# Token-major query/key products with transposes, later S4/S3 sums and spread row scalings in a two-layer hybrid encoder

## The chip, the cores and the metric

The kernel runs on one core of a Trainium2 chip. The metric is the time of one execution on the device in microseconds (us). A profiled execution gives the trace; its time is told beside its span, which goes from the first to the last instruction.

## What is computed

Two layers of a hybrid encoder work on 512 tokens of 2048 features. In each layer the RMS-normalised tokens go through one input projection. Its columns feed a gated linear attention (GLA, 4 heads, with a low-rank forget gate) and a chunked softmax attention (8 heads). Both results are normalised per head, gated, put side by side and multiplied by one output matrix; that product is normalised and added to the tokens. Cut to what matters:

```python
def hybrid_layer(x, ...):
    z = rmsnorm(x, g_pre) @ w_in
    gq, gk, gv, gg, ga, aq, ak, av, ag = split_columns(z)
    o_gla = rmsnorm(gla_chunk_causal(gq, gk, gv, log_a), g_gla) * silu(gg)
    o_att = rmsnorm(chunk_band_attention(aq, ak, av, rel_bias), g_att) * silu(ag)
    y = concatenate([o_gla, o_att]) @ w_out
    return x + rmsnorm(y, g_post)
```

Everything is float32.

## The kernel before, in words

**Numbers.** Each float32 operand is split into a rounded high part and the rest (`split`, L105/L106; with a scale L109/L110: ACT makes the high part, DVE the rest), and a product is the sum of three matmuls: high x high, high x rest, rest x high.

**Products.** The input projection is cut into blocks of 512 columns. Most go in pairs through `fast_gemm` (L316), which forms four block products from seven (P1 to P7, as Strassen does), each over four chunks of 512 rows: 28 jobs a pair. `PAIRS` (L125) gives the order of pairs: two value blocks of attention (AV), two pairs of query/key blocks (QK01/QK23 and QK45/QK67), GK/GQ, GV and GG of the GLA. Then come the output blocks: W01, the first output pair, in both layers, and W23, as a pair in the last layer (L1352) and as plain blocks in the first. The tables L131 to L133 set the order of a pair's jobs; "52" in them is P5 on chunk 2. P1's, P5's and P6's PSUM results are copied by ACT into `ev` tiles (L333), later products are combined with these by DVE (L338).

**A job.** SP issues the loads of weights (L149, `raw` and `H`) and, where needed, of operand sums (L175, `sa`). DVE adds or subtracts weight halves (L185, L187), ACT casts the high part (`wh`, L191), DVE makes the rest (`wl`, L199). Then PE runs its matmuls: 12 of 512 columns token-major (L381), with tokens as the rows of the result, or 24 of 256 columns feature-major (L371), with features as the rows. Only the two query/key pairs are feature-major, since attention wants features there; `qk_consume` splits their results at once, from `ev` or PSUM.

**Order of work.** Besides the products there are tasks, written as Python generators: attention (`attend`, whose steps L929 lists: scores L853 to L855, softmax on DVE L858, transposes L874, mix L891, gate L916), the forget gate, the GLA, the sums for the output pair, the end of the tokens. After each job `pump` (L249) lets the first task take its next steps, as many as the pair's rate says; `until` (L264) pumps until a condition holds. New tasks go to the end of the list, or to its front. From the program so written a scheduler fixes the order on each engine; `tc.issue_after` keeps an instruction behind another.

**Around the output pairs.** `output_sums` makes the operand sums S1, S2, then S4 and S3 of four chunks each (DVE L1136 or L1153, then a split with L105/L106), and in the last layer writes them to DRAM by POOL's DMA for W23. The wait at L1149 sets when an S4 or S3 may be made. W01's results are scaled by the gain (L1281) and their squares summed on ACT (L1280).

**The end of the last layer.** `finish_token` takes the root (DVE L1296, POOL L421), scales the rows of a token block `t` and adds the old tokens `x_mid`. For `t` = 0 and 1 and the first half of `t` = 2 this is ACT (L1305), an accumulating DMA from POOL's queue (L1306) and an output DMA on SP's queue (L1307). The other pieces are one DVE operation (L1311) and an output DMA on SP's or ACT's queue (L1313).

PSUM holds four tiles for products (`mm`) and four for the rest (`ax`).

Of the kernel before, what the change touches and what calls it, by code (L numbers as in the profile page):

```python
# [15 lines left out]
P = 128  # L16
# [10 lines left out]
QS = 128 ** -0.5  # L27
# [6 lines left out]
def hybrid_trunk(  # L34
# [52 lines left out]
    def aux():  # L87
        return ps_ax.tile([P, 512], F32, tag="ax", name=nm("ax"))
# [224 lines left out]
    A = {}  # L313
    roles = ["XY", "YX"]

    def fast_gemm(l, pair, consume, rate=0.0, skip=0, feature_major=False, after=None, end=False, lag=0, ops=A):  # L316
        b0 = pair[0]
        acc = {n: [ps_mm.tile([P, W], F32, tag="mm", name=nm("mm")) for _ in range(2)] for n in roles[0]}
        roles.reverse()
        target = {"P1": "X", "P5": "Y", "P6": "X", "P3": "Y", "P7": "X", "P2": "Y", "P4": "X"}  # L320
        starts = ["P1", "P5", "P2"]
        if end:
            target.update(P2="Z", P4="Y")
            starts.append("P4")
        prod = (PROD_OUT if b0 == NB_IN else PROD_END) if end else PROD
        pace = Pace(rate, skip)
        keep = {}

        def copies(name, src):
            keep[name] = []  # L330
            for t in range(2):
                e = ev()
                nc.scalar.copy(e, src[t])  # L333
                keep[name].append(e)

        def combine(a, b, op, home):
            def f(dst=home):
                nc.vector.tensor_tensor(out=dst, in0=a, in1=b, op=op)  # L338
                return dst
            return f  # L340

        def finished(k, t):
            x_, y_ = acc["X"][t], acc["Y"][t]
            if k == "P3":
                consume(1, 0, t, None, combine(y_, keep["x"][t], ALU.subtract, keep["x"][t]))
            elif k == "P7":
                consume(1, 1, t, None, combine(keep["p5"][t], x_, ALU.subtract, keep["p5"][t]))
            elif k == "P2":
                consume(0, 0, t, None, combine(acc[target[k]][t], keep["p1"][t], ALU.add, keep["p1"][t]))
            elif k == "P4" and end:  # L350
                consume(0, 1, t, None, combine(y_, keep["x"][t], ALU.add, keep["x"][t]))
            elif k == "P4":
                consume(0, 1, t, x_, None)

        def matmuls(job, k, c, ts):
            a = job.a
            if a is None:
                key = {"P1": (0, 0, c), "P2": (1, 0, c), "P4": (1, 1, c)}.get(k) or (LEFT[k], c)
                until(lambda: key in ops)
                a = ops[key]  # L360
            out_ps = acc[target[k]]
            fresh = k in starts and c == 0
            for kk in range(2):
                if feature_major:
                    for ft in range(4):
                        f = slice(ft * P, (ft + 1) * P)
                        tok = slice(kk * 256, (kk + 1) * 256)
                        dst = out_ps[ft // 2][:, (ft % 2) * 256 : (ft % 2 + 1) * 256]
                        terms = ((job.wh, 0), (job.wh, 1), (job.wl, 0))
                        for m, (lhs, part) in enumerate(terms):  # L370
                            nc.tensor.matmul(  # L371
                                dst, lhs[:, kk, f], a[:, part, tok],
                                start=(fresh and kk == 0 and m == 0 and ft % 2 == 0),
                                stop=(c == 3 and kk == 1 and m == 2), skip_group_check=True,
                            )
                else:
                    for t in ts:
                        tok = slice(kk * 256 + t * P, kk * 256 + (t + 1) * P)
                        terms = ((0, job.wh), (0, job.wl), (1, job.wh))
                        for m, (part, rhs) in enumerate(terms):  # L380
                            nc.tensor.matmul(  # L381
                                out_ps[t], a[:, part, tok], rhs[:, kk, :],
                                start=(fresh and kk == 0 and m == 0),
                                stop=(c == 3 and kk == 1 and m == 2), skip_group_check=True,
                            )
# [302 lines left out]
    def layer(l):  # L688
# [272 lines left out]
               (1, 1): ("g12", "g13", "g14", "g15"), (1, 0): ("g4", "g5", "g6", "g7")}  # L961

        def qk_consume(p):
            sets = {}

            def f(j, h, b, src, comb):
# [5 lines left out]
                hs = slice(h * 256, (h + 1) * 256)  # L972
                hi, lo = sets[j][2 * b][:, :, hs], sets[j][2 * b + 1][:, :, hs]
                if b == 0:
                    split_scaled(hi, lo, z, -QS)
# [8 lines left out]
        fast_gemm(l, PAIRS[1], qk_consume(0), rate=2.1, feature_major=True)  # L984
        fast_gemm(l, PAIRS[2], qk_consume(1), rate=2.1, feature_major=True)

        until(lambda: 0 in heads_done)
        tasks.insert(0, forget_gate_decay())
# [137 lines left out]
        def output_sums():  # L1126
# [19 lines left out]
                        yield  # L1146
            for name in ("S4", "S3"):
                for i in range(4):
                    while (("P5", "P6")[i // 2], i % 2 + 2 * (name == "S3")) not in used or (0, OC[i]) not in og:  # L1149
                        yield  # L1150
                    a11, a12, a21, a22 = parts[OC[i]]
                    if name == "S4":
                        nc.vector.tensor_tensor(out=a12, in0=a12, in1=a22, op=ALU.add)  # L1153
                        put(name, i, a12, f"g{i}")
                    else:
                        sub(a11, a11, a21)
                        put(name, i, a11)
                    yield
# [135 lines left out]
        def finish_token(t, xs):  # L1294
# [5 lines left out]
            for i in range(D // step):  # L1300
                h, o = i * step // 1024, i * step % 1024
                yt = ys[t, h][:, o : o + step]
                rows = slice(t * P, (t + 1) * P), slice(i * step, (i + 1) * step)
                if last and (t < 2 or (t == 2 and i == 0)):
                    nc.scalar.activation(yt, yt, AF.Copy, scale=r)  # L1305
                    nc.gpsimd.dma_start(yt, x_mid[rows], accum_op=ALU.add)  # L1306
                    nc.sync.dma_start(out[rows], yt)  # L1307
                else:
                    xt = piece(xs, i * step, step)
                    with tc.issue_after(reduced[3]) if last and t == 2 else nullcontext():  # L1310
                        nc.vector.scalar_tensor_tensor(out=xt, in0=yt, scalar=r, in1=xt, op0=ALU.mult, op1=ALU.add)  # L1311
# [109 lines left out]
```

## Time and profile before

| what | value |
|---|---|
| median of 3 runs | 1646.22 us (1645.83 to 1648.16) |
| the profiled execution | 1642.34 us |
| its span | 1640.5 us |
| granted TensorE clock, mean | 0.995 |
| PE, DVE, ACT busy | 99%, 76%, 55% |

PE is TensorE, DVE VectorE, ACT ScalarE, POOL GpSimd, SP the engine that issues most DMAs; a "q" behind a name means its queue. A row of the timeline gives start, duration, engine, line, operation, written tile <- read tiles and the count; in brackets stands the idle time of that engine ahead of it and what ended it. A row of groups gives busy time and mean duration in ns. A row of the chain in order of time gives start, length and what the chain ran through. Matmuls are pipelined, so the distance between starts, not the duration of one, is its price.

### The profile page before, as it was taken

To read this page: it belongs to the slowest core of one execution; us is meant where nothing else is said; L and a number is where in the kernel's file an instruction comes from. 1 tells how busy PE (TensorE), PEld (TensorE's weight loads), DVE (VectorE), ACT (ScalarE), POOL (GpSimd) and SP (SyncE) were. 2 spreads that over 40 slices of the span, in tenths; PEclk is the share of its full clock that TensorE was granted. 3 is DMA by queue.
4 is the path that set the end of the run, shared out by engine and by line. 5 is a ranking of instruction groups with operands and counts; after the bars stand their busy time and mean duration, and the time that the engine had idled before them with its cause. 6 is when DMAs were issued, how large, how long until landed. Compare 5 with 4: busy or idle time off the path is not lost.

```text
span 1640.5 us, 24563 instructions
## 1 busy us (share of the span) xinstructions
PE 1617.2 (99%) x8986; PEld 1383.7 (84%) x8986; DVE 1253.5 (76%) x1635; ACT 909.7 (55%) x1498; POOL 134.2 (8%) x196
## 2 busy tenths in 40 slices
PE   9999999999999999999999999999999999999996
PEld 7888999998888778788888889999988877787885
DVE  5977677687787869985786576776777878699876
ACT  7554445566555456654784444455665545476554
POOL 0120000110100110000132000000000001101002
PEclk9999999999999999999999999999999999999998
DMA  9898685885859667486789486858758596786968
GB/s 345 270 357 293 221 302 199 266 298 173 307 192 339 225 220 267 145 296 214 240 282 394 172 311 218 298 189 273 269 183 291 184 327 235 241 282 246 345 224 269
DMA packets 130760, 426.70 MB, mean 260 GB/s; under 512 B 14084, under 2 KB 26756, under 8 KB 130640
## 3 DMA queue, kind: packets, MB, share of 16 engines
q1 hardware_dynamic: 113760, 366.09, 64.9%
q0 software_dynamic: 16304, 57.96, 9.7%
q8 instruction: 71, 1.16, 0.3%
q10 hardware_dynamic: 576, 1.08, 0.2%
q14 instruction: 49, 0.40, 0.1%
HBM read 371.84 MB, written 53.23 MB: 259 GB/s over the span
## 4 chain that ended last, share of the span: by engine, by line
PE 94%; DMA 2%; DVE 2%; issue 1%; ACT 0%; SPq 0%; DVEq 0%; POOL 0%; ACTq 0%
PE mm L381 47%; PE mm L371 19%; PE mm L302 16%; PE ax L891 2%; PE ax L381 2%; DMA raw<-in_w_dram 1%; PE ax L1072 1%; PE ax L874 1%; PE ax L711 1%; PE ax L1044 1%; DVE wl L199 1%; PE ax L855 1%; PE ax L854 1%; PE ax L853 1%; PE ax L1164 0%
## 5 line engine op out<-in xcount | busy, mean ns | idle before, releaser
L381 PE MATMUL mm<-wh,sa 128*128 128x512 f32 x1472 | 479.2, 396 | 1.2 <-ACT wh L191 1.0
L191 ACT CAST wh<-raw 128x1024 fp32r<-128x1024 f32 (+1 forms) x253 | 265.1, 1052 | 242.6 <-PE mm L381 65.2
L199 DVE TENSOR_TENSOR wl<-raw,wh 128x1024 fp32r<-128x1024 f32 (+1 forms) x253 | 306.5, 1216 | 92.7 <-PE mm L381 38.3
L191 ACT CAST wh<-H 128x1024 fp32r<-128x1024 f32 x240 | 251.4, 1050 | 214.8 <-PE mm L381 90.2
L199 DVE TENSOR_TENSOR wl<-H,wh 128x1024 fp32r<-128x1024 f32 x240 | 292.5, 1221 | 88.1 <-PE mm L381 35.8
L381 PEld LDWEIGHTS mm<-wh,sa 128*128 128x128 f32 x1472 | 277.5, 189 | 68.9 <-issue 7.9
L381 PE MATMUL mm<-wl,sa 128*128 128x512 f32 x736 | 289.6, 394 | 4.7 <-DVE wl L199 4.7
L371 PE MATMUL mm<-sa,wh 128*128 128x256 f32 x1280 | 236.7, 285 | 0.0
L381 PE MATMUL mm<-wh,a 128*128 128x512 f32 x608 | 200.5, 394 | 0.0
L371 PEld LDWEIGHTS mm<-sa,wh 128*128 128x128 f32 x1280 | 199.7, 191 | 0.1
L371 PE MATMUL mm<-sa,wl 128*128 128x256 f32 x640 | 181.2, 283 | 0.0
L381 PEld LDWEIGHTS mm<-wl,sa 128*128 128x128 f32 x736 | 139.1, 189 | 33.7 <-DVE wl L199 6.7
L185 DVE TENSOR_TENSOR H<-H,raw 128x1024 f32<-128x1024 f32 x132 | 160.2, 1219 | 8.1 <-DMA raw<-in_w_dram 7.0
L381 PEld LDWEIGHTS mm<-wh,a 128*128 128x128 f32 x608 | 113.2, 188 | 23.3
L187 DVE TENSOR_TENSOR raw<-H,raw 128x1024 f32<-128x1024 f32 x60 | 73.5, 1224 | 68.8 <-DMA raw<-in_w_dram 68.7
L371 PEld LDWEIGHTS mm<-sa,wl 128*128 128x128 f32 x640 | 122.5, 191 | 0.2
L421 POOL TENSOR_TENSOR sm<-sm,mhalf 128x2 f32<-128x2 f32 (+2 forms) x42 | 57.1, 1360 | 791.8 <-DVE sm L901 453.3
L381 PE MATMUL mm<-wl,a 128*128 128x512 f32 x304 | 119.8, 394 | 0.0
L371 PE MATMUL mm<-a,wh 128*128 128x256 f32 x512 | 95.2, 285 | 0.0
L302 PE MATMUL mm<-wh,a 128*128 128x512 f32 x288 | 91.7, 390 | 0.0
L381 PE MATMUL mm<-wh,g 128*128 128x512 f32 x288 | 90.8, 389 | 0.0
L333 ACT COPY ev<-mm 128x512 f32<-128x512 f32 x96 | 56.0, 583 | 56.3 <-PE mm L381 39.5
(237 smaller groups left out, 2428.5 us busy)
## 6 DMA issues: line engine op xcount, KB each, us to landing
raw<-in_w_dram SPq DMA_DIRECT2D x323, 512.0 KB, 4.8
sa<-S SPq DMA_DIRECT2D x184, 512.0 KB, 4.4
H<-in_w_dram SPq DMA_DIRECT2D x60, 512.0 KB, 4.6
sa<-A SPq DMA_DIRECT2D x48, 512.0 KB, 5.9
S<-g POOLq DMA_DIRECT2D x32, 512.0 KB, 9.0
sa<-oS SPq DMA_DIRECT2D x16, 512.0 KB, 4.5
oa<-g POOLq DMA_DIRECT2D x12, 512.0 KB, 6.6
bias<-in_rel_dram SPq DMA_DIRECT2D x16, 256.0 KB, 4.2
```

The costliest lines, as they stand in the source:

```text
L185: nc.vector.tensor_tensor(out=h, in0=h, in1=r, op=ALU.add)
L187: nc.vector.tensor_tensor(out=r, in0=h, in1=r, op=ALU.subtract)
L191: last_cast[0] = nc.scalar.copy(self.wh[:, z, :], src[:, z, :]).ins
L199: nc.vector.tensor_tensor(out=self.wl[:, z, :], in0=self.src[:, z, :], in1=self.wh[:, z, :].bitcast(F32), op=ALU.subtract)
L302: nc.tensor.matmul(pss[o], a(part, kk, o) if callable(a) else a[:, part, t], rhs[:, kk, :], start=(i == 0 and kk == 0 and m == 0), stop=(i ...
L333: nc.scalar.copy(e, src[t])
L371: nc.tensor.matmul(dst, lhs[:, kk, f], a[:, part, tok], start=(fresh and kk == 0 and m == 0 and ft % 2 == 0), stop=(c == 3 and kk == 1 and ...
L381: nc.tensor.matmul(out_ps[t], a[:, part, tok], rhs[:, kk, :], start=(fresh and kk == 0 and m == 0), stop=(c == 3 and kk == 1 and m == 2), ...
L421: nc.gpsimd.tensor_tensor(out=out_r, in0=v, in1=mhalf[:, : v.shape[-1]], op=ALU.pow)
L711: nc.tensor.matmul(ps[0:96, half * 256 : (half + 1) * 256], wga[kt // 10][:, kt % 10, :], op[:, i, (kt % 2) * 256 : (kt % 2 + 1) * 256], s ...
L853: nc.tensor.matmul(ps[:, :n], self.qh[:, t], self.kh[:, :n], start=True, stop=False)
L891: nc.tensor.matmul(o, self.pt[i][:, j * P : (j + 1) * P], av[hd // 4, j // 2][:, j % 2, (hd % 4) * P : (hd % 4 + 1) * P], start=(j == 0), ...
```

## The change

It has three parts.

1. The feature-major form is gone. The query/key pairs are computed token-major, like the rest (L368 of the changed kernel). When both token tiles of a block half are there, a new task `turn_qk`, put at the front of the list, waits one step, transposes them with 8 PE transposes into two `ax` tiles, and splits from these. A P4 result, which has no combine, is first copied by ACT into an `ev` tile, 8 copies in all. Attention's task is appended by `turn_qk`, so it starts later.
2. In `output_sums` the wait of S4 and S3 names other jobs: S4 of chunk i waits for P2 on chunk 2 and 3 and P5 on chunk 2 and 3 in turn, S3 besides for P3 on its chunk.
3. In `finish_token` of the last layer the pieces of `t` = 0 and 1 wait three steps each and their ACT scaling stands behind the latest weight cast; the first half of `t` = 2 goes the way of DVE.

```diff
-    def fast_gemm(l, pair, consume, rate=0.0, skip=0, feature_major=False, after=None, end=False, lag=0, ops=A):
+    def fast_gemm(l, pair, consume, rate=0.0, skip=0, after=None, end=False, lag=0, ops=A):
...
-                if feature_major:
-                    for ft in range(4):
-                        f = slice(ft * P, (ft + 1) * P)
-                        tok = slice(kk * 256, (kk + 1) * 256)
-                        dst = out_ps[ft // 2][:, (ft % 2) * 256 : (ft % 2 + 1) * 256]
-                        terms = ((job.wh, 0), (job.wh, 1), (job.wl, 0))
...
+            def turn_qk(j, h, z):
+                yield
+                ps = [aux(), aux()]
+                for b in range(2):
+                    for i in range(2):
+                        for t in range(2):
+                            o = i * 256 + t * P
+                            nc.tensor.transpose(
+                                ps[b][:, o : o + P], z[t][:, (2 * b + i) * P : (2 * b + i + 1) * P], ident
+                            )
+                hs = slice(h * 256, (h + 1) * 256)
+                for b in range(2):
+                    hi, lo = sets[j][2 * b][:, :, hs], sets[j][2 * b + 1][:, :, hs]
+                    v = ps[b].rearrange("p (f n) -> p f n", f=2)
+                    if b == 0:
+                        split_scaled(hi, lo, v, -QS)
+                    else:
+                        split(hi, lo, v)
+                if h:
+                    tasks.append(attend(4 * p + 2 * j, sets[j]))
+                yield
...
-                z = settled(src, comb).rearrange("p (f n) -> p f n", f=2)
...
+                if comb is None:
+                    rows[t] = ev()
+                    nc.scalar.copy(rows[t], src)
                 else:
-                    split(hi, lo, z)
-                if h and b:
-                    tasks.append(attend(4 * p + 2 * j, sets[j]))
+                    rows[t] = comb()
+                if t:
+                    tasks.insert(0, turn_qk(j, h, dict(rows)))
...
-                    while (("P5", "P6")[i // 2], i % 2 + 2 * (name == "S3")) not in used or (0, OC[i]) not in og:
+                    while (("P2", 2), ("P2", 3), ("P5", 2), ("P5", 3))[i] not in used or name == "S3" and ("P3", i) not in used:
...
-                if last and (t < 2 or (t == 2 and i == 0)):
-                    nc.scalar.activation(yt, yt, AF.Copy, scale=r)
+                if last and t < 2:
+                    for _ in range(3):
+                        yield
+                    with tc.issue_after(last_cast[0]):
+                        nc.scalar.activation(yt, yt, AF.Copy, scale=r)
```

The attention steps run later against the products. At the end of the first product of the GV pair, PE's queue stands like this before (L916, L891: attention's gate and mix of its last heads; L381: the product's matmuls; `mm_5022` is the PSUM tile of the next product, P5):

```order
2183 L381 MATMUL mm_5021<-wh_4915,a_107_622 128x512
2184 L916 MATMUL ax_5073<-cst,sg_4683 128x128 x3
2185 L891 MATMUL ax_4973<-g_246_1475,t_911_4971 128x128 x2
2186 L891 MATMUL ax_4973<-g_253_1515,t_911_4971 128x128
2187 L916 MATMUL ax_5073<-cst,sg_4683 128x128
2188 L381 MATMUL mm_5020<-wh_4996,a_113_657 128x512
2189 L381 MATMUL mm_5021<-wh_4996,a_113_657 128x512
2190 L381 MATMUL mm_5022<-wh_4963,sa_4919 128x512
```

Changed, PE's queue at the same place (L861 and L878 are the transposes and mixes, L368 the product's matmuls, `mm_4438` P5's tile):

```order
2032 L368 MATMUL mm_4437<-wh_4481,a_122_698 128x512
2033 L861 MATMUL ax_4357<-cst,t_862_4074 128x128 x4
2034 L861 MATMUL ax_4383<-cst,t_887_4201 128x128 x3
2035 L878 MATMUL ax_4098<-g_246_1475,t_902_4262 128x128
2036 L878 MATMUL ax_4389<-g_246_1475,t_926_4362 128x128 x2
2037 L878 MATMUL ax_4389<-g_253_1515,t_926_4362 128x128 x2
2038 L861 MATMUL ax_4426<-cst,t_899_4256 128x128 x2
2039 L861 MATMUL ax_4459<-cst,t_908_4290 128x128
2040 L878 MATMUL ax_4389<-g_246_1475,t_931_4387 128x128 x2
2041 L878 MATMUL ax_4389<-g_253_1515,t_931_4387 128x128
2042 L368 MATMUL mm_4438<-wh_4379,sa_4335 128x512
```

Where single steps of attention stood among the matmuls of the first product, 18 steps now stand together between its last matmul and P5's first.

In the first output pair of the first layer, DVE's queue around P5 on chunk 2 before (L106: rests of operand sums; L1153, L1136: the sums; L185 and L199: weights; L338, L1281: results of P2):

```order
667 L199 TENSOR_TENSOR wl_6857<-raw_6817,wh_6837 128x1024
668 L106 TENSOR_TENSOR g_1313_6842<-g_1208_6328,g_1313_6842 128x512
669 L106 TENSOR_TENSOR sa_6771<-g_1251_6556,sa_6771 128x512
670 L1153 TENSOR_TENSOR t_1253_6560<-t_1253_6560,t_1255_6562 128x512
671 L1136 TENSOR_TENSOR t_1252_6559<-t_1252_6559,t_1254_6561 128x512
672 L106 TENSOR_TENSOR sa_6775<-t_1255_6562,sa_6775 128x512
673 L185 TENSOR_TENSOR H_6609<-H_6609,raw_6839 128x1024
674 L338 TENSOR_TENSOR t_1327_6927<-ax_6661,ev_6797 128x512
675 L185 TENSOR_TENSOR H_6649<-H_6649,raw_6862 128x1024
676 L1281 TENSOR_TENSOR a_1329_6931<-t_1327_6927,bias_6743 128x512
677 L338 TENSOR_TENSOR t_1331_6935<-ax_6662,ev_6799 128x512
678 L199 TENSOR_TENSOR wl_6880<-H_6609,wh_6860 128x1024
```

Changed (L1143, L1160 and L1288 are L1136, L1153 and L1281):

```order
666 L199 TENSOR_TENSOR wl_6265<-raw_6233,wh_6249 128x1024
667 L1160 TENSOR_TENSOR t_1273_5976<-t_1273_5976,t_1275_5978 128x512
668 L1143 TENSOR_TENSOR t_1272_5975<-t_1272_5975,t_1274_5977 128x512
669 L106 TENSOR_TENSOR sa_6191<-t_1275_5978,sa_6191 128x512
670 L185 TENSOR_TENSOR H_6025<-H_6025,raw_6251 128x1024
671 L338 TENSOR_TENSOR t_1344_6331<-ax_6077,ev_6213 128x512
672 L185 TENSOR_TENSOR H_6065<-H_6065,raw_6270 128x1024
673 L1288 TENSOR_TENSOR a_1346_6335<-t_1344_6331,bias_6159 128x512
674 L338 TENSOR_TENSOR t_1348_6339<-ax_6078,ev_6215 128x512
675 L199 TENSOR_TENSOR wl_6284<-H_6025,wh_6268 128x1024
```

The two L106 with a `g` tile, S4's rests on chunks 0 and 1 (the second is row 668), have gone behind the rows shown; what stands from L185 to the second L338 and its L199 is the same.

At the end of the program, DVE's queue before:

```order
1542 L1296 TENSOR_REDUCE sm_15716<-ssy_15017 128x1
1543 L1281 TENSOR_TENSOR g_3066_15671<-t_3075_15738,t_2951_15129 128x512
1544 L1296 TENSOR_REDUCE sm_15743<-ssy_15025 128x1
1545 L1311 SCALAR_TENSOR_TENSOR g_2946_15118<-g_3063_15665,sm_15717,g_2946_15118 128x1024
1546 L1311 SCALAR_TENSOR_TENSOR bias_15121<-g_2925_15027,sm_15744,bias_15121 128x512
1547 L1311 SCALAR_TENSOR_TENSOR bias_15122<-g_2925_15027,sm_15744,bias_15122 128x512
1548 L1311 SCALAR_TENSOR_TENSOR sg_15123<-g_3066_15671,sm_15744,sg_15123 128x512
1549 L1311 SCALAR_TENSOR_TENSOR sg_15124<-g_3066_15671,sm_15744,sg_15124 128x512
```

Changed:

```order
1540 L1303 TENSOR_REDUCE sm_14548<-ssy_13849 128x1
1541 L1288 TENSOR_TENSOR g_3106_14497<-t_3115_14570,t_2991_13961 128x512
1542 L1303 TENSOR_REDUCE sm_14575<-ssy_13857 128x1
1543 L1321 SCALAR_TENSOR_TENSOR g_2985_13949<-g_2961_13851,sm_14549,g_2985_13949 128x1024
1544 L1321 SCALAR_TENSOR_TENSOR g_2986_13950<-g_3103_14491,sm_14549,g_2986_13950 128x1024
1545 L1321 SCALAR_TENSOR_TENSOR bias_13953<-g_2965_13859,sm_14576,bias_13953 128x512
1546 L1321 SCALAR_TENSOR_TENSOR bias_13954<-g_2965_13859,sm_14576,bias_13954 128x512
1547 L1321 SCALAR_TENSOR_TENSOR sg_13955<-g_3106_14497,sm_14576,sg_13955 128x512
1548 L1321 SCALAR_TENSOR_TENSOR sg_13956<-g_3106_14497,sm_14576,sg_13956 128x512
```

One 1024-column operation is added at the front of the last ones; the matching ACT scaling and POOL DMA are gone, and SP's output of that piece moved ahead of the 512-column ones.

More of the change, by code (lines that the diff above doesn't have):

```diff
@@ L363, in matmuls @@
             for kk in range(2):
-                if feature_major:
-                    for ft in range(4):
-                        f = slice(ft * P, (ft + 1) * P)
-                        tok = slice(kk * 256, (kk + 1) * 256)
-                        dst = out_ps[ft // 2][:, (ft % 2) * 256 : (ft % 2 + 1) * 256]
-                        terms = ((job.wh, 0), (job.wh, 1), (job.wl, 0))
[L370 to L385, printed above, removed]
+                for t in ts:
+                    tok = slice(kk * 256 + t * P, kk * 256 + (t + 1) * P)
+                    terms = ((0, job.wh), (0, job.wl), (1, job.wh))
+                    for m, (part, rhs) in enumerate(terms):
+                        nc.tensor.matmul(
+                            out_ps[t], a[:, part, tok], rhs[:, kk, :],
+                            start=(fresh and kk == 0 and m == 0),
+                            stop=(c == 3 and kk == 1 and m == 2), skip_group_check=True,
+                        )
         for k, c in prod:
@@ L963, in qk_consume, with f @@
         def qk_consume(p):
-            sets = {}
-            def f(j, h, b, src, comb):
+            sets, rows = {}, {}
+            def turn_qk(j, h, z):
[7 more added lines that the diff above has]
+                                ps[b][:, o : o + P], z[t][:, (2 * b + i) * P : (2 * b + i + 1) * P], ident
+                            )
+                hs = slice(h * 256, (h + 1) * 256)
[9 more added lines that the diff above has]
+                yield
+            def f(j, h, t, src, comb):
                 if j not in sets:
@@ L970, in f @@
                     sets[j] = [slot(tag, [2, 512], F32R) for tag in QKT[p, j]]
-                z = settled(src, comb).rearrange("p (f n) -> p f n", f=2)
[L972 to L975, printed above, removed]
-                else:
-                    split(hi, lo, z)
-                if h and b:
-                    tasks.append(attend(4 * p + 2 * j, sets[j]))
+                if comb is None:
+                    rows[t] = ev()
+                    nc.scalar.copy(rows[t], src)
+                else:
+                    rows[t] = comb()
+                if t:
+                    tasks.insert(0, turn_qk(j, h, dict(rows)))
             return f
@@ L983, in layer @@
         load_bias(1)
-        fast_gemm(l, PAIRS[1], qk_consume(0), rate=2.1, feature_major=True)
-        fast_gemm(l, PAIRS[2], qk_consume(1), rate=2.1, feature_major=True)
+        fast_gemm(l, PAIRS[1], qk_consume(0), rate=2.1)
+        fast_gemm(l, PAIRS[2], qk_consume(1), rate=2.1)
         until(lambda: 0 in heads_done)
```

## The prediction

> **What bounds the kernel now.** I read the page first: the busy times, then the chain of work that ended last.
>
> ```profile
> PE 1617.2 (99%) x8986; PEld 1383.7 (84%) x8986; DVE 1253.5 (76%) x1635; ACT 909.7 (55%) x1498; POOL 134.2 (8%) x196
> PE 94%; DMA 2%; DVE 2%; issue 1%; ACT 0%; SPq 0%; DVEq 0%; POOL 0%; ACTq 0%
> ```
>
> TensorE (PE) is busy nearly always and owns 94% of the chain, so a change counts where it changes PE's own work, where PE waits, or behind PE's last matmul. Work that ACT or DVE gains or loses costs nothing while PE stays fed. The waits of PE, with total, times and longest, name the one place where it isn't:
>
> ```profile
> PE mm L381 <- DVE wl L199: 5.0, 3, 2.3
> ```
>
> The timeline finds it in the first output pair of each layer (at 682 us in the first). Besides PE's own work and this wait, the tail behind the last matmul counts. The sum has a part for each place that the change touches.
>
> **Query/key products: 112 jobs and 16 batches.** The chain in order of time (start, us, what) prices both forms of a job, the value pair first and the query/key pairs second:
>
> ```profile
> 102.76 76.16 PE mm L381 x336
> 178.92 65.03 PE mm L371 x542
> ```
>
> That is 76.16/336 = 0.2267 us for a 512-column matmul and 65.03/542 = 0.1200 for a 256-column one, both without holes. A job of 24 narrow ones takes 2.880, of 12 wide ones 2.720. Two pairs of 28 jobs in two layers are 112 jobs: 112 x 0.160 = **-17.9 us**.
>
> The new transposes: 8 to a batch, one batch for each of 4 block halves, 2 pairs and 2 layers: 16 batches, 128 transposes. The same chain has transposes of the same shape out of the same kind of tile (ev, L995), and groups of four between narrow and between wide matmuls:
>
> ```profile
> 324.14 0.44 PE ax L874 x4
> 324.57 2.87 PE mm L371 x24
> ...
> 409.17 0.44 PE ax L874 x4
> 409.61 2.75 PE mm L381 x12
> ...
> 446.57 0.87 PE ax L995 x8
> ```
>
> A batch is 0.87; a batch cut into 4 and 4 is 0.88. With a hundredth or two for each join I take 0.89: 16 x 0.89 = **+14.2** (bounds 13.9 and 14.6). The foreign groups that stand in these pairs already will stand between wide matmuls: 24 narrow ones behind a group took 2.87 for 2.88, 12 wide ones 2.75 for 2.72. So a group costs between 0 and 0.04 more; the changed order has about 40 a layer. I take 0.012, a third of the upper end, since most groups are longer than this one and closer together: 80 x 0.012 = **+1.0** (0 to 3.2). This part is -2.7.
>
> Its cover: PE waits for the combine L338 or the new copies before a batch, and other matmuls stand there. The 8 copies cost 8 x 583 ns = 4.7 us of ACT, and the splits now read PSUM. The windows of a query/key stage (columns: window, length, then busy us of PE, PEld, DVE, ACT, POOL) show room on both:
>
> ```profile
> L333 ACT COPY ev<-mm 128x512 f32<-128x512 f32 x96 | 56.0, 583 | 56.3 <-PE mm L381 39.5
> 179.00:246.00 67.00, 67.00 (x559) 66.92 (x557) 48.93 (x46) 30.54 (x35) 0.00 (x0) 1.00 0.75 256
> 246.00:370.00 124.00, 124.00 (x1025) 123.12 (x1024) 92.72 (x164) 74.79 (x162) 10.87 (x12) 1.00 0.75 254
> ```
>
> DVE is 75% busy at most, ACT 60%. If a batch had no cover, PE would wait for one combine, about 0.7 each, 11 us in all; I cost this at nothing.
>
> One rule speaks against the part. The Trainium skill, "TensorE: Matmul & The Clock Gate", section "Back-to-back issue gap", gives N/2.4 + 2.5 ns for an isolated matmul of N columns: by it (an estimate) 24 narrow ones take 2.62 us, 12 wide ones 2.59, and the 112 jobs would save 3, not 18. The chain's rows above disagree with that for narrow matmuls (0.120, not 0.109) and the trace decides.
>
> **The start of the value pair (GV).** The order rows in the section on the change show 18 small attention instructions in a row between GV's first product and P5, most of them waiting for ACT or DVE; before, such steps stood among matmuls. Behind them comes P5's first matmul, whose PSUM tile comes free when DVE has read the last GK product (L1016). DVE prices, from before's rows at the same place:
>
> ```profile
> 361.41 0.69 DVE L338 TENSOR_TENSOR ev<-mm,ev 128x512 f32<-128x512 f32 x1 [1.19 <-PE mm L371]
> 362.18 1.23 DVE L199 TENSOR_TENSOR wl<-H,wh 128x1024 fp32r<-128x1024 f32 x1
> 363.32 0.68 DVE L338 TENSOR_TENSOR ev<-mm,ev 128x512 f32<-128x512 f32 x1
> 363.93 0.41 DVE L858 CUSTOM_DVE_ANT_0 t<-ax,bias 128x256 f32<-128x256 f32 x1
> 364.26 1.22 DVE L185 TENSOR_TENSOR H<-H,raw 128x1024 f32<-128x1024 f32 x1
> 365.40 0.68 DVE L110 SCALAR_TENSOR_TENSOR g<-ev,g 128x512 fp32r<-128x512 f32 x1
> ```
>
> Starts lie 1.14 apart behind L199 and L185 and 0.6 behind a 512-column operation. From the combine of GK's P2 to the L1016 of its P4 the changed DVE queue holds 14 of the first (16.0), 8 of the second (4.9) and about 4 us of small ones: 25 us. PE has 72 wide matmuls (16.3) and 72 small ones (0.11 to 0.23, 8.6) there: 25 us as well. They meet with nothing to spare, so any gap of DVE becomes a wait. I take 1.0 a layer, a gap like the 1.19 in the first row: **+2.0** (0.3 to 3 a layer).
>
> **S4 and S3 of the first output pair.** DVE and PE at the wait:
>
> ```profile
> 680.68 1.22 DVE L185 TENSOR_TENSOR H<-H,raw 128x1024 f32<-128x1024 f32 x1
> 681.96 0.69 DVE L338 TENSOR_TENSOR t<-ax,ev 128x512 f32<-128x512 f32 x1
> 682.57 1.22 DVE L185 TENSOR_TENSOR H<-H,raw 128x1024 f32<-128x1024 f32 x1
> 683.70 0.68 DVE L1281 TENSOR_TENSOR a<-t,bias 128x512 f32<-128x512 f32 x1
> 684.30 0.68 DVE L338 TENSOR_TENSOR t<-ax,ev 128x512 f32<-128x512 f32 x1
> 684.90 1.22 DVE L199 TENSOR_TENSOR wl<-H,wh 128x1024 fp32r<-128x1024 f32 x1
> ...
> 683.11 0.73 PE L381 MATMUL mm<-wh,sa 128*128 128x512 f32 x2 [0.51 <-ACT wh L191]
> 686.17 0.50 PE L381 MATMUL mm<-wl,sa 128*128 128x512 f32 x1 [2.33 <-DVE wl L199]
> ...
> 688.91 1.48 PE L381 MATMUL mm<-wh,sa 128*128 128x512 f32 x3
> 690.19 0.63 PE L381 MATMUL mm<-wl,sa 128*128 128x512 f32 x1
> 691.31 0.62 PE L381 MATMUL mm<-wh,sa 128*128 128x512 f32 x2
> ```
>
> In the order rows two splits (L106, 0.6 each) have left the queue ahead of P5's L185, so that comes 1.2 earlier and its cast too. But L338 starts at 681.96 behind PE's P2, which ends no earlier, and L185, L1281, L338 still stand between it and the wl that PE lacks. PE goes on at 686.17 as before: **0**. Behind the wait three wide matmuls take 690.19 - 688.91 = 1.28, 0.43 each instead of 0.227; the timeline has about eight of these up to 691.3, some 1.6 us lost. Whether a hole of another shape still brings that is open: -1.6 to +1.6 a layer.
>
> **The tail.** Last DVE, POOL and SP rows, then the DMA rate of 1627 to 1632, and the load in 40 slices of 1636.6 to 1640.5:
>
> ```profile
> 1627.18 1.28 DVE L1311 SCALAR_TENSOR_TENSOR g<-g,sm,g 128x1024 f32<-128x1024 f32 x1 [0.17 <-POOL sm L421]
> 1628.38 1.41 DVE L1311 SCALAR_TENSOR_TENSOR bias<-g,sm,bias 128x512 f32<-128x512 f32 x2
> 1628.70 0.88 POOL L1306 DMA_DIRECT2D g<-x_mid  x1 [1.04 <-ACT g L1305]
> 1617.61 0.85 POOL L1306 DMA_DIRECT2D g<-x_mid  x1
> 1627.82 0.33 SPq L1307 DMA_DIRECT2D out_dram<-g  x1
> 1636.66 0.33 SPq L1307 DMA_DIRECT2D out_dram<-g  x1
> ...
> DMA packets 597, 2.01 MB, mean 401 GB/s; under 512 B 73, under 2 KB 73, under 8 KB 597
> ...
> DMA  9999643109989899899998100000000000000000
> ...
> L191 ACT CAST wh<-H 128x1024 fp32r<-128x1024 f32 x240 | 251.4, 1050 | 214.8 <-PE mm L381 90.2
> ```
>
> The accumulating DMA of the third token block, issued at 1628.70, holds the last output back to 1636.66, and that moves until about 1638.9. The change takes this DMA off POOL and gives DVE one more 1024-column L1311: DVE then ends 1.2 later, at 1627.18 + 2 x 1.20 + 4 x 0.70 = 1632.4. Outputs of 2.5 MB (t=1's last piece onward) at 401 GB/s from 1628.5 end at 1634.7. Two weight casts put ahead of the last two L1305 (1.05 each, the last row) make t=1's pieces at most 2.1 later; then SP, whose queue holds them ahead of the rest, starts at 1629.9 and ends near 1636.1. The end comes 2.8 to 4.2 earlier; I take **-3.5** (0 if t=1's piece itself lands near 1636).
>
> **Sum.** -2.7 + 2.0 + 0 - 3.5 = -4.2 on the profiled execution's 1642.34 (span 1640.5), so 1638.1. The median of the runs shown lies 3.88 above that execution, at 1646.22: 1646.22 - 4.2 = 1642.0.
>
> **Rivals.**
> - *PE waits at GV* (slower). The price above decides: if DVE comes 3 us late in each layer, and the slow matmuls follow as they did behind 2.33 us at 686, 4.6 a layer replace 1.0: -2.7 + 9.2 - 3.5 = +3.0, 1649.2. It turns slower than before from 3.1 a layer. For it: the balance of 25 against 25. Against: elsewhere the queues hide such bursts. 0.17.
> - *The tail is hidden*: t=1's pieces, delayed, land as late as the third block did. -0.7, 1645.5. For it: t=1's last piece already took from 1617.61's issue to 1627.82. 0.15.
> - *The wait at 682 goes* after all, because DVE has two splits less: 0.51 + 2.33 of wait and 1.6 of slow matmuls a layer, -8.9 more: 1633.1. Against it: the unchanged order behind L338. It is also the case in which the edit does what its words say. 0.07.
> - *No saving from width*: the wide matmuls of these pairs run at 0.240 instead of 0.2267, because their operands are other tiles; the first part is then +15.2 instead of -2.7, 1659.9. The chain of 336 wide ones without a hole speaks against it. 0.03. By the rule of the Trainium skill above (an estimate) nearly the same would follow, from narrow ones that are as good.
>
> **How the numbers follow.** Forecast 0.55 (own range 1638.5 to 1645.5), the rest 0.03. A measurement tells 0.2%, 3.3 us, from no change: below 1642.9 or above 1649.5. The forecast gives 0.34 faster and 0.21 same; the tail rival 0.13 same, 0.02 faster; GV 0.14 slower, 0.03 same; the wait 0.07 faster; width 0.03 slower; the rest 0.01 each. Faster 0.44, same 0.38, slower 0.18. The range 1637.0 to 1649.5 leaves out the wait, width, and the upper part of GV: under 0.2.
>
> **What would show it.** The query/key jobs at 2.72 and batches at 0.9 in the chain; no wait of PE on L338 or the copies; at GV's P5 a wait on L1016 (L1023 there) of about 1 us; the wait on wl in the first output pair unchanged near 3; the last SP output issued by 1632 and the end about 1637 on before's clock. A wait above 3 us at GV or in front of the batches would make me wrong upward, a vanished wl wait downward.

## The result and the profile after

The changed kernel takes 1648.53 us (median of 20 runs, 1645.98 to 1655.19), before 1645.60 (20 runs, 1641.31 to 1650.80). The ratio is 1.0021, with a 95% interval of 1.0011 to 1.0030: slower by about 3.4 us, where 4.2 us faster was forecast. The profiled execution of the changed kernel took 1648.88 us with a span of 1647.1, close to its median; that of before was 3.3 us faster than its own, so the two traces differ by 6.5 us, about twice the medians' difference. Stages are therefore compared over several kernels below, not over this pair alone. Executions in a second, slower state, e3's profiled one among them (1778.90 us at a granted clock of 0.848), are left out of the ratios below, and e3's trace isn't used.

The page of the changed kernel still shows an engine that is nearly always busy. The longest rows of its waits of PE (total, times, longest) follow; before had no counterpart of the second, and 1.0, 2, 0.5 for the third:

```profile
PE 1619.0 (98%) x7770; PEld 1329.2 (81%) x7770; DVE 1256.7 (76%) x1636; ACT 910.9 (55%) x1505; POOL 131.8 (8%) x195
```

```profile
PE mm L368 <- DVE wl L199: 6.5, 2, 3.4
PE ax L878 <- ACT t L864: 2.8, 2, 1.4
PE mm L368 <- ACT wh L191: 2.2, 1, 2.2
```

L368, L878 and L864 are L381, L891 (attention's mix) and L877 (ACT's copy of a transpose) of before. The second row is the wait at GV, the third a single wait near the end of the first output pair of layer 1.

**Where the time went.** I cut each trace at the first matmul of the first query/key pair and at the first one of GG. In this stretch lies all work of the first part of the change, wherever the scheduler put it. Windows (from:to, length, busy us of PE, PEld, DVE, ACT and POOL, clock, DMA share, GB/s), layers 0 and 1, before and then changed:

```profile
178.76:555.29 376.53, 376.53 (x2498) 341.56 (x2496) 284.47 (x403) 210.14 (x379) 24.00 (x26) 1.00 0.73 252
996.75:1372.02 375.27, 375.03 (x2498) 341.51 (x2496) 281.57 (x395) 208.04 (x371) 19.71 (x22) 1.00 0.73 247
```

```profile
178.35:556.10 377.75, 375.48 (x1890) 312.50 (x1889) 284.83 (x403) 211.27 (x383) 23.84 (x26) 1.00 0.74 251
998.30:1376.60 378.30, 376.67 (x1890) 312.74 (x1889) 282.78 (x395) 208.34 (x375) 20.65 (x22) 1.00 0.72 245
```

The stretch is 1.2 and 3.0 us longer, 4.2 in all, where the prediction had -2.7 + 2.0 = -0.7. PE is idle for 2.3 and 1.6 us in it, before for 0 and 0.2. The rest of the traces' difference is +4.0 in the output pairs of both layers (3.2 of it in the first output pair of layer 1), -0.4 ahead of the stretch, and -1.3 in the tail.

**The wait at GV.** Rows of the changed kernel's timeline at the place that the order rows of the change showed (others in between are left out):

```profile
477.56 1.05 ACT L191 CAST wh<-H 128x1024 fp32r<-128x1024 f32 x1
478.13 0.39 PE L878 MATMUL ax<-g,t 128*128 128x128 f32 x2
478.52 0.58 ACT L333 COPY ev<-mm 128x512 f32<-128x512 f32 x1
479.26 0.58 ACT L864 COPY t<-ax 128x512 f32<-128x512 f32 x1
479.89 1.16 PE L878 MATMUL ax<-g,t 128*128 128x128 f32 x8 [1.38 <-ACT t L864]
480.27 1.28 DVE L1023 TENSOR_TENSOR t<-mm,g 128x512 f32<-128x512 f32 x2
482.20 0.48 PE L368 MATMUL mm<-wh,sa 128*128 128x512 f32 x1
```

PE has nothing but attention's 18 instructions to run. Its mix at 479.89 waits 1.38 us for ACT's copy of the transposes, and that stands in ACT's queue behind a weight cast and a copy of GV's first product. DVE's L1023, which is before's L1016 that the prediction had named, has read PSUM by 481.55, before P5 starts at 482.20. It was not far behind, though: DVE's next rows follow without a hole from 477.34 to 481.55, so with a faster copy on ACT alone PE could have met L1023 instead. No run separates the two. In the first output pair the wait for wl is still there, as one hole (in layer 1):

```profile
1507.48 0.50 PE L368 MATMUL mm<-wl,sa 128*128 128x512 f32 x1 [3.12 <-DVE wl L199]
```

**The tail.** Rows of DVE and SP in the changed kernel's tail:

```profile
1635.00 2.48 DVE L1321 SCALAR_TENSOR_TENSOR g<-g,sm,g 128x1024 f32<-128x1024 f32 x2 [0.18 <-POOL sm L408]
1637.31 0.33 SPq L1317 DMA_DIRECT2D out_dram<-g  x1
1637.73 0.38 SPq L1323 DMA_DIRECT2D out_dram<-g  x1
1638.20 0.86 SPq L1323 DMA_DIRECT2D out_dram<-bias  x1
1639.50 0.85 SPq L1323 DMA_DIRECT2D out_dram<-sg  x1
```

The output that waited until 1636.66 is no longer last. But SP holds t=1's last piece (L1317) until 1637.31, 2.31 us behind the start of DVE's first 1024-column row shown; before it was 0.64 behind. The tail from the start of the last matmul to the end is 14.7 us, before 15.9.

### The profile page after: what moved, and what is told of

It reads as the page before. It is cut to its first block, busy times and chain, and to the rows that moved or that the text cites. A ratio compares the mean times of both kernels' runs of the same rounds, so it can differ in the third digit from the quotient of the medians.

```text
span 1647.1 us, 22095 instructions
## 1 busy us (share of the span) xinstructions
PE 1619.0 (98%) x7770; PEld 1329.2 (81%) x7770; DVE 1256.7 (76%) x1636; ACT 910.9 (55%) x1505; POOL 131.8 (8%) x195
## 5 line engine op out<-in xcount | busy, mean ns | idle before, releaser
L368 PE MATMUL mm<-wh,sa 128*128 128x512 f32 x2112 | 685.0, 396 | 0.4 <-DMA sa<-S 0.4
L368 PEld LDWEIGHTS mm<-wh,sa 128*128 128x128 f32 x2112 | 397.6, 189 | 90.6 <-issue 8.2
L368 PE MATMUL mm<-wl,sa 128*128 128x512 f32 x1056 | 417.4, 395 | 6.5 <-DVE wl L199 6.5
L199 DVE TENSOR_TENSOR wl<-raw,wh 128x1024 fp32r<-128x1024 f32 (+1 forms) x253 | 306.6, 1216 | 86.8 <-PE mm L368 47.2
L199 DVE TENSOR_TENSOR wl<-H,wh 128x1024 fp32r<-128x1024 f32 x240 | 292.4, 1220 | 101.4 <-PE mm L368 62.1
L368 PE MATMUL mm<-wh,a 128*128 128x512 f32 x864 | 284.1, 394 | 0.0
L368 PEld LDWEIGHTS mm<-wl,sa 128*128 128x128 f32 x1056 | 200.0, 189 | 47.1 <-DVE wl L199 7.3
L368 PEld LDWEIGHTS mm<-wh,a 128*128 128x128 f32 x864 | 161.0, 188 | 32.6
L368 PE MATMUL mm<-wl,a 128*128 128x512 f32 x432 | 170.7, 395 | 0.0
L185 DVE TENSOR_TENSOR H<-H,raw 128x1024 f32<-128x1024 f32 x132 | 160.4, 1221 | 10.8 <-DMA raw<-in_w_dram 9.3
L368 PEld LDWEIGHTS mm<-wl,a 128*128 128x128 f32 x432 | 81.3, 188 | 16.5
L368 PE MATMUL mm<-wh,g 128*128 128x512 f32 x288 | 91.1, 390 | 2.2 <-ACT wh L191 2.2
L302 PE MATMUL mm<-wh,a 128*128 128x512 f32 x288 | 91.8, 390 | 0.0
L302 PE MATMUL mm<-wh,g 128*128 128x512 f32 x240 | 82.0, 392 | 0.0
L204 DVE TENSOR_TENSOR H<-H,raw 128x1024 f32<-128x1024 f32 x48 | 58.6, 1222 | 23.9 <-DMA raw<-in_w_dram 23.8
L302 PE MATMUL mm<-wh,sa 128*128 128x512 f32 x224 | 73.5, 394 | 0.0
L368 PEld LDWEIGHTS mm<-wh,g 128*128 128x128 f32 x288 | 54.1, 188 | 13.8 <-ACT wh L191 2.7
```

The lines of the kernel that those rows point to most:

```text
L185: nc.vector.tensor_tensor(out=h, in0=h, in1=r, op=ALU.add)
L199: nc.vector.tensor_tensor(out=self.wl[:, z, :], in0=self.src[:, z, :], in1=self.wh[:, z, :].bitcast(F32), op=ALU.subtract)
L204: nc.vector.tensor_tensor(out=h, in0=h, in1=self.src, op=ALU.add)
L302: nc.tensor.matmul(pss[o], a(part, kk, o) if callable(a) else a[:, part, t], rhs[:, kk, :], start=(i == 0 and kk == 0 and m == 0), stop=(i ...
L368: nc.tensor.matmul(out_ps[t], a[:, part, tok], rhs[:, kk, :], start=(fresh and kk == 0 and m == 0), stop=(c == 3 and kk == 1 and m == 2), ...
```

## The experiments

After the result I had three causes to tell apart: the first part by itself (and in it the width, the transposes and attention's lateness), the later sums, and the pacing in the tail. Ratios are to before, on the same chip, with 95% intervals. All of them are small beside the spread of single executions (before: 1641.3 to 1650.6 over 35 runs).

### Each part alone, and two together

`e1_qk_only` is before with part 1, `e2_sums_only` with part 2, `e3_tail_only` with part 3, `e4_qk_and_tail` is the changed kernel with before's S4/S3 wait:

```diff
e1, e4: -  while (("P2", 2), ("P2", 3), ("P5", 2), ("P5", 3))[i] not in used or ...
e1, e4: +  while (("P5", "P6")[i // 2], i % 2 + 2 * (name == "S3")) not in used or ...
e1:     -  if last and t < 2:  (three yields, scaling behind the last cast)
e1:     +  if last and (t < 2 or (t == 2 and i == 0)):
e2:     the sums' wait of the change, put into before
e3:     the tail's condition, yields and issue_after of the change, put into before
```

> Only part 1 (token-major query/key pairs with transposes). From the stages of the two traces: the query/key pairs 15 us shorter, GK/GQ and GV 19 us longer in sum (attention moved there, 1.83 us of waiting per layer on ACT's copy L864), so +3 to +4 us. By the prediction's working it would be -0.7 us.

Measured: 1648.47 us, ratio 1.0019 (1.0006 to 1.0032), +3.1 us. The stretch took 377.9 and 379.0 us, 5.1 more than before, with the same wait of 1.4 us at GV in both layers. The first part alone is as slow as the whole change. The traces had led to +3 to +4, the prediction's working to -0.7.

> Only part 2 (later S4/S3). If the new wait of 2.4 us on a weight cast in the last pair of layer 1, with slow matmuls behind it, comes from the later sums and their DRAM writes, it is here too: +3 to +5 us, all of it in the output pair of layer 1. Rival: the wait needs the other parts' shift in time, or only chance of the clock: 0 here, as predicted.

Measured: 1645.23 us, ratio 0.9991 (0.9981 to 1.0002). No wait on a weight cast at the end of that pair; the first output pair takes 83.0 us in layer 1, before 84.0. So my reading of the trace after, that the later sums and their DRAM writes bring the wait on the cast, fell; the prediction's 0 stands. At P5 on chunk 2, where before waited 0.51 + 2.33 us, it waits once:

```profile
1502.86 0.50 PE L381 MATMUL mm<-wl,sa 128*128 128x512 f32 x1 [3.12 <-DVE wl L199]
```

> Only part 3 (scaled rows). The changed kernel's trace has 14.7 us behind the start of the last matmul where before had 15.9: -1.3 us. The prediction took -3.5, with 0 as the other end.

Measured: 1643.39 us, ratio 0.9984 (0.9972 to 0.9995), -2.6 us with an uncertainty of 1.9. That holds both -1.3 and -3.5, and rules out 0.

> Parts 1 and 3 without part 2. If the parts add up: +3.5 - 1.3 = about +2 us, with the first output pair of layer 1 back at 84.0 us (87.2 in the changed kernel) and no wait on a weight cast there. If part 2's cost is a chance of the clock, this is as slow as the changed kernel.

Measured: 1650.03 us, ratio 1.0015 (1.0006 to 1.0024), +2.5, near the +2 expected. The single runs of parts 1 and 3 add up to +0.5, below this interval (+1.0 to +4.0) but within their own uncertainty. The first output pair of layer 1 took 88.3 us without part 2 (87.0 in e1), more than the changed kernel's 87.2; waits on wl stand there in e1, at other places than in the changed kernel:

```profile
1531.10 0.51 PE L368 MATMUL mm<-wl,g 128*128 128x512 f32 x1 [1.01 <-DVE wl L199]
1547.05 0.50 PE L368 MATMUL mm<-wl,g 128*128 128x512 f32 x1 [1.79 <-DVE wl L199]
```

Over twelve kernels (before, the changed one and ten of these) this pair took 82.8 to 88.3 us in one profiled execution each, 82.8 to 87.2 with the later sums and 83.6 to 88.3 with the old ones. So the +3.2 us that the pair of traces showed there doesn't belong to part 2. The three that took 87.0 or more are the three with part 1 as the change has it; no run says why. Whether these waits, which end with a late weight, are a habit of some kernels or of single executions is open: each kernel was profiled once.

### The pace of attention

```diff
-        fast_gemm(l, PAIRS[1], qk_consume(0), rate=2.1)
-        fast_gemm(l, PAIRS[2], qk_consume(1), rate=2.1)
+        fast_gemm(l, PAIRS[1], qk_consume(0), rate=2.4)
+        fast_gemm(l, PAIRS[2], qk_consume(1), rate=2.4)
```

The new task takes two steps per block half, eight per pair; 2.4 instead of 2.1 steps in each of 28 jobs gives attention eight back.

> The changed kernel with 2.4 instead of 2.1 task steps per job in the two query/key pairs, which makes up for the steps that the new task takes from attention. If the wait in GV (1.43 + 0.29 us a layer at attention's mixes) comes from attention being late, it goes, and the stretch from the first query/key pair to GG falls from 377.7 and 378.3 us by 1.5 to 2 a layer: -3 us against the changed kernel, about as fast as before. Rival: the wait comes from DVE's load in that stretch, wherever attention stands; then it stays or moves and the stretch stays within 0.5 us.

Measured: 1642.70 us, ratio 0.9977 (0.9968 to 0.9985): -3.8 us against before and some 7 against the changed kernel. The stretch:

```profile
178.66:554.79 376.13, 376.13 (x1889) 312.70 (x1888) 285.45 (x403) 213.65 (x383) 24.48 (x26) 1.00 0.73 252
999.20:1373.02 373.82, 373.82 (x1889) 312.94 (x1888) 283.34 (x395) 210.15 (x375) 18.78 (x22) 1.00 0.73 248
```

PE is busy for all of it, and at the start of GV attention's steps stand among the product's matmuls again. The stretch is 1.6 and 4.5 us shorter than in the changed kernel, 6.1 in both layers, where 3 to 4 were expected: 3.9 of them are PE's idle time, the other 2.2 lie in small losses between its matmuls. It is 1.9 shorter than before. DVE's work there is the same to 1.2 us, so DVE's load as a whole, the rival, is not the cause. Other kernels agree, both layers together: 756.0 to 756.9 us with part 1 at 2.1 (changed, e1, e4), 750.0 to 752.1 at 2.4 (e5, e9, e10), 751.5 to 753.7 with before's pairs (before, e2, e7, e8).

The chain of e5 also shows the price of a wide query/key matmul; the row runs from the value pair (336 matmuls) into the first query/key pair:

```profile
102.31 130.16 PE mm L368 x572
```

That is 0.2276 us each, 2.73 for a job of 12.

The counter-test slows attention in before, which has neither the new transposes nor wide query/key matmuls (`e11_before_slow_pace`). It takes 0.4 steps in each of 28 jobs, 11 a pair, somewhat more than the 8 of the new task:

```diff
-        fast_gemm(l, PAIRS[1], qk_consume(0), rate=2.1, feature_major=True)
-        fast_gemm(l, PAIRS[2], qk_consume(1), rate=2.1, feature_major=True)
+        fast_gemm(l, PAIRS[1], qk_consume(0), rate=1.7, feature_major=True)
+        fast_gemm(l, PAIRS[2], qk_consume(1), rate=1.7, feature_major=True)
```

> Before, with 1.7 instead of 2.1 task steps per job in its two query/key pairs and nothing else changed. Its queue on PE then has the same 18 attention instructions in a row ahead of P5 of GV. If late attention by itself makes the wait, PE waits there 1.4 us or more a layer on ACT's copy (L877), and the stretch from the first query/key pair to GG grows from 376.5 and 375.3 by 2 to 3 us a layer: +4 to +6 us. If the wait needs the transposes or the wide matmuls, it stays within 1 us of before.

Measured: 1650.64 us, ratio 1.0026 (1.0011 to 1.0041), +4.3 us. Its stretches, and rows of PE and ACT in GV of layer 0:

```profile
178.74:557.98 379.24, 376.32 (x2498) 341.81 (x2496) 284.50 (x403) 210.26 (x379) 22.35 (x26) 1.00 0.73 250
1001.58:1379.04 377.46, 376.41 (x2498) 341.58 (x2496) 282.90 (x395) 207.30 (x371) 21.05 (x22) 1.00 0.72 246
```

```profile
480.01 0.39 PE L891 MATMUL ax<-g,t 128*128 128x128 f32 x2
481.14 0.58 ACT L877 COPY t<-ax 128x512 f32<-128x512 f32 x1
481.77 1.16 PE L891 MATMUL ax<-g,t 128*128 128x128 f32 x8 [1.38 <-ACT t L877]
```

The stretch grows by 2.7 and 2.2 us with not one instruction added, PE's busy time stays within 1.4, and in layer 0 the same 1.38 us stand at the same copy. In layer 1 product matmuls stood among the steps and PE did not wait at that place; it waited 0.33 and 0.72 us at another mix and a gate of attention, and layer 0 has two more such waits, 0.62 and 0.71. So the expectation of 1.4 in each layer held in one of them. Late attention alone makes a slowdown of this size.

### The width without the transposes

```diff
-                ps = [aux(), aux()]
-                for b in range(2):
-                    ...
-                            nc.tensor.transpose(...)
-                    v = ps[b].rearrange("p (f n) -> p f n", f=2)
+                    v = z[b].rearrange("p (f n) -> p f n", f=2)
```

> The changed kernel without the 128 transposes; the splits read the token-major rows as if they were feature-major, so the attention works on other numbers and its output is another; the steps of the task stay. Prices the width alone: if wide matmuls save 17.9 us and only joins and the GV wait are lost, the stretch from the first query/key pair to GG is 8.9 + ... less than before by about 6 us a layer (370 us), -11 to -12 us in all against before. If the width saves only 3 us, it is within 3 us of before.

Measured: 1634.90 us, ratio 0.9929 (0.9916 to 0.9941), -11.7 us. The stretch:

```profile
178.44:548.18 369.74, 367.76 (x1826) 306.22 (x1824) 283.79 (x403) 211.26 (x383) 24.85 (x26) 1.00 0.74 256
990.85:1362.72 371.87, 369.56 (x1825) 306.35 (x1824) 280.78 (x395) 209.30 (x375) 20.58 (x22) 1.00 0.73 249
```

It is 10.2 us shorter than before, although attention is as late as in the changed kernel and PE waits 1.9 us at GV in each layer (3.7 in all on ACT's copy). Without these waits it would be 13.9 shorter: the 17.9 predicted for the width, less a remainder of some 4. The prediction had +1.0 for joins in its place; that all of the remainder is joins isn't shown. By the isolated gap that the Trainium skill gives in "TensorE: Matmul & The Clock Gate", section "Back-to-back issue gap", the saving would be 3 us (the prediction's estimate); the measurement decides against it, and against the rival without a saving. The transposes are the difference to the changed kernel: 756.05 - 741.61 = 14.4 us for both stretches, with nearly equal waits at GV in both; predicted 14.2.

### The tail, and the best version

`e7_third_block_only` is before with the condition changed to `t < 2` and nothing else; `e8_sums_third_block` adds part 2:

```diff
-                if last and (t < 2 or (t == 2 and i == 0)):
+                if last and t < 2:
```

> Before with only the third token block's first half moved to DVE; the other scalings stay where they were. The tail rows of the changed kernel say that t=1's last piece, 1.7 us later because of the pacing, holds SP back and costs that gain: without pacing the end comes 1.5 to 2 us earlier than with it, -2.8 to -3.5 us against before. If the pacing is harmless, it is -1.3 to -2.6, as the whole of part 3.

Measured: 1643.23 us, ratio 0.9981 (0.9969 to 0.9993), -3.1 us. Rows of its tail:

```profile
1631.22 2.48 DVE L1311 SCALAR_TENSOR_TENSOR g<-g,sm,g 128x1024 f32<-128x1024 f32 x2 [0.18 <-POOL sm L421]
1631.96 0.33 SPq L1307 DMA_DIRECT2D out_dram<-g  x1
1632.54 0.33 SPq L1313 DMA_DIRECT2D out_dram<-g  x1
1634.40 0.33 SPq L1313 DMA_DIRECT2D out_dram<-bias  x1
```

SP sends t=1's last piece 0.74 us behind the start of DVE's row of 1024 columns, not 2.31, and the tail is 12.9 us, 3.0 shorter than before. Over the kernels, the tail takes 15.6 to 16.9 us without part 3 (before, e1, e2, e11), 14.7 to 15.9 with it (changed, e4, e5, e6), and 12.3 to 14.8 with the third block moved and no pacing (e7 to e10). In these single profiled executions the pacing gave away most of the gain. The runs show only 0.5 us of it (e3 against e7, e5 against e9), which isn't told from nothing, and the -3.1 of e7 holds both expectations.

> Before with the later S4/S3 sums and the third block on DVE without pacing: a candidate to beat both. The single runs of part 2 (0.9991) and the last expectation add up to -4 to -5 us, 1641 to 1642.

Measured: 1642.81 us, ratio 0.9975 (0.9965 to 0.9985), -4.1 us, as expected, with a tail of 12.3.

`e9_pace_unpaced_tail` is e5 with this tail; `e10_same_old_sums` is e9 with before's sums:

```diff
e9, e10: +  rate=2.4 in both query/key pairs
e9, e10: -  for _ in range(3): yield; with tc.issue_after(last_cast[0]):
e10:     +  before's wait of S4 and S3
```

> The changed kernel with 2.4 steps per job in the query/key pairs and the scalings of t = 0 and 1 where before had them (only the third block's first half moved to DVE). If the three causes found so far add up (first part -1.9, sums about 0, third block -3.0 to -3.7), it is -5 to -6 us against before, faster than every kernel so far. If the faster pace and the tail share one gain, it stays at -4.

Measured: 1641.24 us, ratio 0.9974 (0.9961 to 0.9986), -4.3 us. Of the two expectations the smaller gain, -4, is nearer; -5 to -6 lies inside the interval too. In its profiled execution t=1's last piece was late all the same (SP sent it 2.27 us behind DVE's start), and the tail took 14.8.

> The last kernel without part 2 (S4 and S3 as before). Theory: part 2 is worth nothing, so within 1.5 us of the last one. Rival, from the first single run of part 2 (0.9991): part 2 gains 1 to 1.5 us and this is slower by that.

Measured: 1644.29 us, ratio 0.9984 (0.9973 to 0.9995), -2.6 us. 1.6 us slower than e9 by the ratios, with overlapping intervals. The four pairs of kernels that differ in part 2 alone put it at -1.5 (e2), -1.0 (e8 against e7), -1.6 (e9 against e10) and +1.0 us (changed against e4): it isn't told from nothing.

E9, e8 and e5 are the fastest versions that compute the same result, 0.26, 0.25 and 0.23% faster than before, and by the ratios 0.47, 0.46 and 0.44% faster than the changed kernel; their intervals overlap. E8 has nothing of the first part. Nor do the pairs that differ in the first part at 2.4 alone show a gain of it: e9 against e8 0.9974 to 0.9975, e10 against e7 0.9984 to 0.9981. The 1.9 us in e5's stretch are of one trace, and whole runs don't tell the restored first part from nothing.

## Why the prediction was wrong

- **Width and transposes: right in mechanism and near in size.** An uninterrupted job took 2.73 us in e5 for the predicted 2.720, and the transposes cost 14.4 for 14.2. That batches have cover held but for one hole of 0.33 us in layer 0 of the changed kernel's trace, ahead of a transpose that waits for L338. With attention's pace restored (e5) the first part is -1.9 us in the stretch, for the -2.7 predicted.
- **The failed step: what late attention costs.** "I take 1.0 a layer, a gap like the 1.19 in the first row" gave +2.0, for the start of GV alone and for DVE. The changed kernel and e5 differ in attention's pace only, and the stretch by 6.1 us: 3.9 of PE's idle time, 3.0 of it at the start of GV (1.38 + 0.13 a layer), and 2.2 between matmuls. E11 prices a somewhat later attention without any other edit: +4.9 in the stretch, +4.3 us (0.26%) in the runs. The prediction also had the releaser wrong: ACT's copy in a queue behind a cast and a product's copy ends the wait, not DVE's L1016, though that came close behind. What the order rows showed, 18 dependent instructions with no matmul of a product between, was the point itself; the balance of 25 us of DVE against 25 us of PE was not what decided.
- **Joins: too small in the changed kernel.** "I take 0.012, a third of the upper end" gave +1.0. What is left of the stretch without waits, width and transposes is about 4 in the changed kernel and e6, about 1.9 in e5 (its -1.9 against -17.9 + 14.2), inside the 0 to 3.2 given. With equal matmuls it is smaller where attention isn't late, so it isn't joins alone; 2.2 of it are counted in the step above.
- **Sums: right.** PE goes on at the same time, 38.2 to 38.6 us behind the start of the pair in layers 0 and 1 of twelve traces; 0.51 + 2.33 us of wait became 3.12 to 3.36. Slow matmuls still follow in most (last section).
- **Tail: right in mechanism, too large.** "I take **-3.5**" allowed t=1's pieces to come 2.1 us later, and they came 1.7 later (2.31 against 0.64 behind DVE's start); but the outputs from there on took 8.0 us (1637.31 to 1645.32) and not the 6.2 of 2.5 MB at 401 GB/s, and -3.5 lay in the middle between the branch with that delay (-2.8) and one without it. Measured: -1.3 in the pair of traces and -3.0 in e7's, without pacing; in the runs -2.6 (e3) and -3.1 (e7), each with an uncertainty of some 2.
- **The sum.** In the pair of traces PE's losses without a wait are 3.3 us more than predicted, the waits of the stretch 1.7 more, and the tail 2.2 more: -4.2 becomes +3.0. The 4.0 in the output pairs, which the prediction had at nothing, are tied to no part of the change by any run. Measured is +3.4 by the ratio; with single traces that scatter by 2 us a stage this agreement is partly luck. The rival "PE waits at GV" with its 1649.2 was the nearest of the cases, though it took 4.6 us a layer for DVE's lateness and slow matmuls, and neither was seen there.

## What to carry to other kernels

When work is inserted ahead of a task list that is pumped at a fixed rate, count the steps that it takes from the tasks behind it, and raise the rate by as much; here 0.3 steps a job was worth 7 us, more than the edit itself. A run of small dependent instructions on the bounding engine, with no independent work among it, can become a wait even where the engines that feed it have time to spare on average: look whose queue its copies stand in. An edit that gains 2% of a stage by shape and gives it back by transposes is decided by many small losses, here 1.9 to 4 us over 112 jobs, so price those from several rows of both kinds before the large terms.

## What the runs showed of the hardware

PE's granted clock fell to 0.5 in or behind holes of 1.8 to 3.5 us, and stayed there for 3.4 us (before, 687.7 to 691.1) or 6.8 (changed, 685.9 to 692.8); which of the two followed no visible rule. Behind 3.36 us of wait in the changed kernel's layer 0, wide matmuls came 0.43 us apart from 687.8 to 692.5, at a granted clock of 0.50 (rows left out in between):

```profile
687.23 0.80 PE L368 MATMUL mm<-wl,sa 128*128 128x512 f32 x1 [3.36 <-DVE wl L199]
...
691.24 1.48 PE L368 MATMUL mm<-wh,sa 128*128 128x512 f32 x3
...
692.87 0.40 PE L368 MATMUL mm<-wh,sa 128*128 128x512 f32 x1
```

That is 2.2 us lost, before 1.6 behind 0.51 + 2.33. E10 has the same two waits as before in layer 0, its clock stays at 1.00 and none of its matmuls behind them is slow; e4 in layer 0 and e6 in layer 1 are like it. So such a hole can cost more than half as much again as it shows, in one execution and not in the next.

The accumulating DMAs of 512 KB from POOL's queue at the end of the program took 5.5 to 11.7 us from their issue to the output that waited for them, in e9 11.7 (1623.15 to 1634.84), before 10.2 and 8.0. The plain output DMAs of the same size whose landing the traces show took 2.6 to 5.7.
